# Order of the first loads, and where the second mixer's residual comes from, in a two-layer hybrid encoder kernel

## Chip, cores and metric

The kernel runs on one core of one Trainium2 chip. The metric is the device time of one execution in microseconds (us); lower is better. A profiled execution gives the trace from which all rows below are read.

## The reference

The stream x is 1024 tokens by 1024 channels. Two layers are applied, A and B, and a last norm. Each layer is

```
h = rmsnorm(x)
z = h @ w_in                       # token mixer and 4 memory-attention heads from one projection
x = x + concat(token_mixer(z), memory_attention(z, mem)) @ w_out
x = x + conv_ffn(rmsnorm(x))
...
out = rmsnorm(x)
```

Layer A's token mixer is a gated block of width 768 (u times a spatially mixed v, with a bias `a_b_s`). After layer A one shared K and V and a forget gate (with a bias `b_f` for each of 12 heads) are computed from x. Layer B's token mixer is causal attention with that K, V and a decay. The line that matters most here is the first residual of layer B: the x that is added to the mixer's output is the stream that left layer A's feed-forward part.

## The kernel before

All products are done in float32 precision with split operands: a tile is cast to a rounded high part (ScalarE, ACT) and the remainder is the low part (VectorE, DVE, or GpSimd, POOL): `split_to` (L346, L347), `wconv` for weights (L213 multiplies the gains in, L217 casts, L218 subtracts). TensorE (PE) then runs three products for each pair. Tiles of 128 x 1024 come from one pool of 33 buffers called X.

The program is written as straight code, and a planner orders each engine's instructions by its own model of times. Matmuls are pinned to the order in which they are written while `strict` is set. A load made with `ld` (L184) is pinned behind the load written before it on the same queue as long as `dpin` is set; a load that is not pinned may be moved ahead of loads that were written earlier, if nothing holds it. Nearly all loads and stores are issued from SP's queue, one after the other; a few small ones of the start are issued from ACT's.

**Start.** Written in this order: two tiles of x, the rows of norm gains (on ACT's queue), two weights of the first projection (`ast.load(2)`), six more tiles of x, two of mem, `ws_raw`; then `dpin` is cleared. In a loop over four pairs of x tiles, `x_in(i+1)` transposes and splits the next pair, and `vv_g` multiplies the pair before with the first weight. The first call of `vv_g` asks for the third weight (`m`, 0) too. The bias `bsb` (L1121, eight small broadcasts) and `bf` (L1225, one) are written much later, and not pinned.

**End of layer A.** `ffn` ends with `out_phase`; when a tile of the new stream is whole, `on_done` calls `done_a`, which splits it into `nh`, `nl` and adds its square to a sum. They become `xh`, `xl`, the operands of layer B's projections. `xdram` is a DRAM array that holds the stream in the middle of each layer (`mix_out` writes it, L577, and `load_xT` reads it).

**End of layer B's attention.** After 48 attention steps, `tail` loads the six attention outputs `o` from DRAM (L1607, tiles of the ring `nb`, three buffers), splits each (`split_new`), and between them `merge_next` (L1599) adds `xl` and `xh` on GpSimd to get the residual back. The memory attention runs at the same time: `mem_s` (reduce L478, exponential L481, reciprocal L484, and `normalise` L459 on GpSimd) and `mem_p` (transpose, split, product). `mix_part` multiplies the split `o` with the output weight and adds the residual (L565).

Of the kernel before, what the change touches and what calls it, by code (L numbers as in the profile page):

```python
# [13 lines left out]
ALU = mybir.AluOpType  # L14
AX = mybir.AxisListType

P = 128
# [42 lines left out]
def kernel(  # L60
# [33 lines left out]
    nc = tc.nc  # L94
# [8 lines left out]
    xdram = dp.tile([D, S], F32, name="xdram")  # L103
# [9 lines left out]
    def nm(s):  # L113
        uid[0] += 1
        return f"{s}_{uid[0]}"

    def xt_(dt=F32, shape=(P, S)):
        return xp.tile(list(shape), dt, tag="X", name=nm("X"))
# [7 lines left out]
    def small(n, tag="sm", p=P):  # L126
        return sm.tile([P, n], F32, tag=tag, name=nm(tag))[:p]
# [3 lines left out]
    def f32(ap):  # L131
        return ap.bitcast(F32)
# [48 lines left out]
    dpin = [False]  # L181

    def ld(dst, src):
        ins = nc.sync.dma_start(dst, src)  # L184
        if dpin[0]:
            tc.keep_in_program_order(ins)
# [100 lines left out]
    def proj_tm_g(ws, xh, xl, j, res, width=256):  # L287
        ps = pa()[:, :width]
        res.append(ps)
        for k in range(KT):  # L290
            wh, wl = ws[k // 4]
            for i, (a, b) in enumerate(((xh, wh), (xh, wl), (xl, wh))):
                mm(
                    ps, a[k][:, j * P:(j + 1) * P], b[:, k % 4, :],
                    start=(k == 0 and i == 0), stop=(k == KT - 1 and i == 2),
                )
            yield 324


    def rpow(dst, src, n):  # L300
        nc.gpsimd.tensor_tensor(dst, src, mhalf[:, :n], ALU.pow)
# [31 lines left out]
    def add_square(tp, ssum, src, n, tag="T", bufs=None):  # L333
        if n == 0:
            nc.scalar.activation(ssum, src, AF.Square)
        else:
            sq = tp.tile([P, S], F32, tag=tag, name=nm("sq"), bufs=bufs)
            nc.scalar.activation(sq, src, AF.Square)
            if n == KT - 1:
                nc.vector.tensor_tensor(ssum, ssum, sq, ALU.add)  # L340
            else:
                nc.gpsimd.tensor_tensor(ssum, ssum, sq, ALU.add)

    def split_to(hi, lo, src, g=None):
        if g is None:
            nc.scalar.copy(hi, src)  # L346
            nc.vector.tensor_tensor(lo, src, f32(hi), ALU.subtract)  # L347
        else:
            nc.scalar.activation(hi, src, AF.Copy, scale=g)
            nc.vector.scalar_tensor_tensor(lo, src, g, f32(hi), ALU.mult, ALU.subtract)  # L350

    def split_new(t):
        hi, lo = xt_(F32R), xt_(F32R)
        split_to(hi, lo, t)
        return hi, lo
# [8 lines left out]
    def mem_norm(tp, mtok, jtag, jbufs):  # L364
        rm = small(2, "rt")
        ms = small(2)
        for t in range(2):
            junk = tp.tile([P, D], F32, tag=jtag, name=nm("jk"), bufs=jbufs)
            nc.scalar.activation(junk, mtok[t], AF.Square, accum_out=ms[:, t:t + 1])
        ms2 = small(2)  # L370
        nc.vector.tensor_scalar(ms2, ms, 1.0 / D, EPS, ALU.mult, ALU.add)
        rpow(rm, ms2, 2)
        return rm
# [143 lines left out]
    def drain(g):  # L517
        for _ in g:
            pass
# [32 lines left out]
    def mix_part(ww, ks, mh, ml, xn):  # L552
        wh, wl = ww
        ps = [pa(), pa()]
        for k in ks:
            for i, (a, b) in enumerate(((wh, mh), (wh, ml), (wl, mh))):
                for c in range(NC2):
                    mm(
                        ps[c], a[:, k, :], b[k][:, c * CH:(c + 1) * CH],
                        start=(k == ks[0] and i == 0), stop=(k == ks[-1] and i == 2),  # L560
                    )
                yield 432
        for c in range(NC2):
            cs = slice(c * CH, (c + 1) * CH)
            nc.vector.tensor_tensor(xn[:, cs], ps[c], xn[:, cs], ALU.add)  # L565
# [435 lines left out]
    xh = [xt_(F32R) for _ in range(KT)]  # L1001
    xl = [xt_(F32R) for _ in range(KT)]
    r_a = small(8, "rt")

    def x_in(i):
        ss, s2 = small(2), small(2)
        toks = xtok[2 * i:2 * i + 2]
        for j in range(2):
            junk = tp.tile([P, S], F32, tag="P", name=nm("jk"), bufs=pbufs[0])
            nc.scalar.activation(junk, toks[j], AF.Square, accum_out=ss[:, j:j + 1])  # L1010
        nc.vector.tensor_scalar(s2, ss, 1.0 / D, EPS, ALU.mult, ALU.add)
        rpow(r_a[:, 2 * i:2 * i + 2], s2, 2)
        for k2 in range(KT // 2):
            ps = pa()
            for k in range(2):
                for j in range(2):
                    kk = 2 * k2 + k
                    tr(ps[:, (2 * k + j) * P:(2 * k + j + 1) * P], toks[j][:, kk * P:(kk + 1) * P], ident)
            for k in range(2):
                cs = slice(2 * i * P, (2 * i + 2) * P)  # L1020
                split_to(xh[2 * k2 + k][:, cs], xl[2 * k2 + k][:, cs], ps[:, 2 * k * P:(2 * k + 2) * P])
# [29 lines left out]
    ws_raw = tp.tile([P, 4, P], F32, tag="T2", name="ws_raw", bufs=3)  # L1051
    ld(ws_raw, a_w_s[0].rearrange("g t s -> t g s"))

    dpin[0] = False
    vg = {}
    sv = cp.tile([P, KT, 3], F32, name="sv")

    def vv_square(cc, j):
        junk = tp.tile([P, CH], F32, tag="T2", name=nm("jk"), bufs=t2b[0])
        nc.scalar.activation(  # L1060
            junk[:, :256], vg[cc, j // 4][:, j % 4, :], AF.Square, accum_out=sv[:, j, cc:cc + 1])

    def vv_g(cc, js):
        ws = ast.use(("v", cc), 2)
        for j in js:
            if j % 4 == 0:
                vg[cc, j // 4] = xt_(F32, (P, 4, 256))
            res = []
            yield from proj_tm_g(ws, xh, xl, j, res)
            d = vg[cc, j // 4][:, j % 4, :]  # L1070
            nc.scalar.activation(  # L1071
                d, res[0], AF.Gelu_apprx_tanh if cc == 0 else AF.Copy, scale=r_a[:, j:j + 1])
            if cc == 0:
                vv_square(cc, j)

    for i in range(4):
        if i < 3:
            x_in(i + 1)
        drain(vv_g(0, (2 * i, 2 * i + 1)))
    rm = mem_norm(tp, mtok, "P", pbufs[0])  # L1080
    rb = cp.tile([P, S], F32, name="rb_a", tag="rb", bufs=1)

# [33 lines left out]
    bsb = tp.tile([P, 6, P], F32, tag="bsb", name="bsb", bufs=1)  # L1116
    fgroups = [[(0, 0, P)], [(0, 0, 64), (1, 64, P)], [(1, 0, P)],
               [(2, 0, P)], [(2, 0, 64), (3, 64, P)], [(3, 0, P)]]
    for f in range(6):
        for g, lo_, hi_ in fgroups[f]:  # L1120
            ld(bsb[lo_:hi_, f, :], a_b_s[0, g:g + 1, :].broadcast_to([hi_ - lo_, P]))  # L1121

    memq.append(mem_q(1))

# [76 lines left out]
    xT = {}  # L1201
# [20 lines left out]
        return a[:, :n], a[:, n:], b[:, :n], b[:, n:]  # L1222

    bf = cp.tile([P, 12], F32, name="bf")
    nc.sync.dma_start(bf, b_f.rearrange("(o h) -> o h", o=1).broadcast_to([P, 12]))  # L1225
    nh, nl, ssums = [], [], []

    def done_a(n, xn):
        h, l = xt_(F32R), xt_(F32R)
        split_to(h, l, xn)  # L1230
        nh.append(h)
        nl.append(l)
        if n == 0:
            ssums.append(tp.tile([P, S], F32, tag="T", name=nm("S"), bufs=4))
        add_square(tp, ssums[0], xn, n, "T", 4)
# [7 lines left out]
    def before_last(stage):  # L1243
# [11 lines left out]

    ffn(ops, ssum_a, first, a_ffn_out[0], lambda: conv_cols("cva", a_ffn_conv, a_ffn_conv_b),
        done_a, tp, False, before_last)
    drain(mt_g[0])
    ssum, = ssums
    xh, xl = nh, nl  # L1260
# [194 lines left out]
    for pr in range(5):  # L1455
        p = PSEQ[pr + 1]
        eng = nc.vector if pr == 0 else None
        wst.add(("k", p), *ntile_src(w_kv, p * P), g_kv, None, eng, pr == 0)
        wst.add(("q", p), *ntile_src(w_q, p * P), g_b1, None, eng, pr == 0)
        if pr in (1, 3):  # L1460
            g = GSEQ[(pr + 1) // 2]
# [89 lines left out]
    for pr in range(5):  # L1551
        fills.append((proj_kq(PSEQ[pr + 1]), KQ, 0, 8 * pr + KQD))
        if pr in (1, 3):
            g = GSEQ[(pr + 1) // 2]
# [38 lines left out]

    xT = {}

    def merge_next(eng):
        n = NORD[len(xT)]
        t = xt_()
        eng.tensor_tensor(t, f32(xl[n]), f32(xh[n]), ALU.add)  # L1599
        xT[n] = t  # L1600

    mix = {}

    def tail():
        for i, p in enumerate(PSEQ):
            o = tp.tile([P, S], F32, tag="nb", name=nm("o"), bufs=3)
            nc.sync.dma_start(o, odram[p * P:(p + 1) * P, :])  # L1607
            if i < 5:
                merge_next(nc.gpsimd)
            mix[p] = split_new(o)  # L1610
        while len(xT) < KT:
            merge_next(nc.gpsimd)
        mh, ml = ({p: mix[p][i] for p in PSEQ} for i in range(2))
        for n in NORD[:NPRE]:
            yield from mix_part(wst.use(("o", n), 1)[0], PSEQ, mh, ml, xT[n])

    tg = tail()
    debt = 0.0
    for cost in mem_g:
# [73 lines left out]
```

## Time and profile before

| what | value |
|---|---|
| runs of the kernel | 2258.61 us median of 3 (2258.33 to 2260.14) |
| the profiled execution, own time | 2259.49 us |
| its span, first to last instruction | 2257.7 us |
| PE busy | 2140.5 us, 95% of the span |
| DVE, ACT, POOL busy | 1719.6, 1036.4, 794.0 us |
| granted clock of PE, mean | 0.987 |

The span is what the trace covers; the execution's own time is 1.79 us longer. In the rows below, a time at the start of a line is us from the start of the span; PEld is PE's weight load, SPq and ACTq are the issuing of a transfer by that queue, not the transfer. "[7.23 <-DMA X<-in_x_dram]" at the end of a row says that the engine was idle for 7.23 us before it and that this transfer ended the wait.

### The profile page before, as it was taken

The numbers are of one execution on the slowest core, as the hardware profiler recorded it, in microseconds if no ns is written. First come the engines' busy times: TensorE is split into PE (matmuls) and PEld (weight loads), VectorE is DVE, ScalarE is ACT, GpSimd is POOL, SyncE is SP. The second block draws the span as 40 slices with busy tenths as digits, with TensorE's granted clock in tenths as the row PEclk, the third lists the DMA queues.
The fourth block names the chain that finished last, engine by engine and source line by source line (L and its number), as shares of the span: only waits on it lengthen the run. The fifth ranks groups of instructions, "written<-read, shape, count | busy, mean of one in ns | idle before, by whom it ended". The sixth has DMA issues, their size and how long they took to land.

```text
span 2257.7 us, 29405 instructions
## 1 busy us (share of the span) xinstructions
PE 2140.5 (95%) x10657; PEld 1785.8 (79%) x10657; DVE 1719.6 (76%) x2544; ACT 1036.4 (46%) x1732; POOL 794.0 (35%) x602
## 2 busy tenths in 40 slices
PE   7999999999999999999899999789999999999998
PEld 6997877778777888878788788667777778788886
DVE  4745667888888899566776766785888888887965
ACT  6562344444434434344565555654434444445433
POOL 1311543333333100351545554555333333320023
PEclk9999999999999999999999999999999999999999
DMA  5310322222222675513332333323222222248563
GB/s 175 100 29 29 93 95 66 72 78 85 84 78 81 225 273 177 169 34 93 104 79 81 88 103 81 96 84 103 68 75 84 71 79 84 85 160 278 159 198 120
DMA packets 219165, 243.54 MB, mean 108 GB/s; under 512 B 10074, under 2 KB 155648, under 8 KB 219020
## 3 DMA queue, kind: packets, MB, share of 16 engines
q1 hardware_dynamic: 218880, 241.63, 34.3%
q8 instruction: 84, 1.38, 0.3%
q14 instruction: 61, 0.50, 0.1%
q10 hardware_dynamic: 140, 0.04, 0.0%
HBM read 192.29 MB, written 38.85 MB: 102 GB/s over the span
## 4 chain that ended last, share of the span: by engine, by line
PE 66%; DVE 18%; issue 6%; ACT 5%; POOL 3%; DMA 3%; ACTq 0%; DVEq 0%; POOLq 0%; SPq 0%
PE pa L137 59%; PE pc L137 5%; DVE X L701 4%; DVE X L699 4%; PE pc L143 2%; DVE ws L660 1%; DVE P L1378 1%; DMA nb<-cdram 1%; DVE U L720 1%; DVE X L347 1%; POOL wo L641 1%; DVE X L430 1%; ACT P L1384 1%; POOL wl L218 1%; DVE PTl L347 1%
## 5 line engine op out<-in xcount | busy, mean ns | idle before, releaser
L137 PE MATMUL pa<-X,wo 128*128 128x512 f32 x3696 | 856.8, 392 | 27.1 <-DVE U L720 21.0
L137 PEld LDWEIGHTS pa<-X,wo 128*128 128x128 f32 x3696 | 691.7, 188 | 189.9 <-DVE U L720 37.6
L137 PE MATMUL pa<-X,X 128*128 128x512 f32 (+2 forms) x1868 | 440.1, 379 | 14.3 <-DVE sm L1378 9.1
L137 PEld LDWEIGHTS pa<-X,X 128*128 128x128 f32 x1868 | 340.0, 189 | 83.3 <-DVE sm L1378 9.1
L137 PE MATMUL pa<-X,wh 128*128 128x512 f32 (+1 forms) x1216 | 354.9, 401 | 10.6 <-DVE X L347 8.5
L641 POOL TENSOR_TENSOR wo<-raw,wo 128x512 fp32r<-128x512 f32 x132 | 223.8, 1695 | 319.2 <-ACT wo L639 315.6
L137 PEld LDWEIGHTS pa<-X,wh 128*128 128x128 f32 x1216 | 219.9, 191 | 56.2 <-DVE X L347 11.0
L639 ACT CAST wo<-ws 128x512 fp32r<-128x512 f32 x176 | 109.3, 622 | 300.8 <-PE pa L137 293.3
L798 ACT CAST X<-ro 128x1024 fp32r<-128x1024 f32 (+1 forms) x142 | 131.0, 965 | 175.8 <-DVE ro L806 74.0
L641 POOL TENSOR_TENSOR wo<-ws,wo 128x512 fp32r<-128x512 f32 x88 | 116.3, 1321 | 233.5 <-ACT wo L639 226.9
L137 PE MATMUL pa<-X,wl 128*128 128x512 f32 (+1 forms) x608 | 195.6, 401 | 2.6 <-POOL wl L218 2.5
L799 POOL TENSOR_TENSOR X<-ro,X 128x1024 fp32r<-128x1024 f32 (+1 forms) x24 | 59.5, 2482 | 344.8 <-ACT X L798 336.2
L218 POOL TENSOR_TENSOR wl<-wr,wh 128x1024 fp32r<-128x1024 f32 (+1 forms) x41 | 104.0, 2538 | 183.6 <-ACT wh L217 178.6
L137 PE MATMUL pa<-wh,X 128*128 128x256 f32 (+1 forms) x800 | 167.4, 287 | 0.5 <-ACT X L1071 0.5
L799 DVE TENSOR_TENSOR X<-ro,X 128x1024 fp32r<-128x1024 f32 (+1 forms) x118 | 142.6, 1237 | 31.6 <-ACT X L798 29.2
L137 PEld LDWEIGHTS pa<-wh,X 128*128 128x128 f32 x800 | 132.3, 189 | 2.3 <-ACT X L1071 0.7
L137 PEld LDWEIGHTS pa<-X,wl 128*128 128x128 f32 x608 | 111.0, 191 | 23.0 <-POOL wl L218 2.9
L639 ACT CAST wo<-raw 128x512 fp32r<-128x512 f32 x132 | 81.3, 616 | 95.0 <-PE pa L137 90.3
L347 DVE TENSOR_TENSOR PTl<-pc,PTh 128x512 fp32r<-128x512 f32 (+1 forms) x152 | 90.9, 602 | 36.7 <-ACT PTh L346 35.2
L137 PE MATMUL pa<-wl,X 128*128 128x256 f32 (+1 forms) x400 | 113.6, 284 | 2.2 <-POOL wl L218 2.2
L1384 ACT ACTIVATE P<-P,sm 128x128 f32<-128x128 f32 (+3 forms) x96 | 74.8, 779 | 77.8 <-DVE sm L1378 75.9
L459 POOL TENSOR_SCALAR P<-P,sm 128x128 f32<-128x128 f32 (+3 forms) x96 | 76.3, 795 | 92.6 <-DVE sm L1385 81.4
(196 smaller groups left out, 3337.9 us busy)
## 6 DMA issues: line engine op xcount, KB each, us to landing
ro<-hdram SPq DMA_DIRECT2D x67, 512.0 KB
raw<-in_a_ffn_in_dram SPq DMA_DIRECT2D x44, 512.0 KB
hdram<-X SPq DMA_DIRECT2D x44, 512.0 KB
raw<-in_b_ffn_in_dram SPq DMA_DIRECT2D x44, 512.0 KB
ro<-in_a_ffn_out_dram SPq DMA_DIRECT2D x35, 512.0 KB
ro<-in_b_ffn_out_dram SPq DMA_DIRECT2D x32, 512.0 KB
X<-X SPq DMA_DIRECT2D x80, 128.0 KB
xdram<-X SPq DMA_DIRECT2D x16, 512.0 KB
```

The source lines that it names most:

```text
L137: ins = nc.tensor.matmul(*a, **k)
L143: ins = nc.tensor.transpose(*a)
L218: eng.tensor_tensor(lo, raw, f32(hi), ALU.subtract)
L347: nc.vector.tensor_tensor(lo, src, f32(hi), ALU.subtract)
L459: nc.gpsimd.tensor_scalar(p, p, rinv, 1.0, ALU.mult, ALU.mult)
L639: nc.scalar.copy(h, src)
L641: eng.tensor_tensor(l, src, f32(h), ALU.subtract)
L699: nc.vector.scalar_tensor_tensor(t[:, 1:], h[:, :S - 1], w1, t[:, 1:], ALU.mult, ALU.add)
L701: nc.vector.scalar_tensor_tensor(t[:, 2:], h[:, :S - 2], w0, t[:, 2:], ALU.mult, ALU.add)
L798: nc.scalar.copy(h, src)
L799: (nc.gpsimd if pool else nc.vector).tensor_tensor(l, src, f32(h), ALU.subtract)
L1384: nc.scalar.activation(p[:, :n], p[:, :n], AF.Exp, bias=mn, scale=-1.0, accum_out=rs)
```

## The change

Five edits. The pinning of loads lasts until after the loop over x. The eight broadcasts of `bsb` are issued from ACT's queue, pinned behind what is written before them there (the key splits of the memory attention). `bf` is pinned behind what is written before it on SP's queue. `done_a` stores each finished tile to `xdram`. `tail` loads the residual from `xdram` where it was added up on GpSimd.

```diff
-    dpin[0] = False
     vg = {}
     sv = cp.tile([P, KT, 3], F32, name="sv")
@@
         if i < 3:
             x_in(i + 1)
         drain(vv_g(0, (2 * i, 2 * i + 1)))
+    dpin[0] = False
     rm = mem_norm(tp, mtok, "P", pbufs[0])
@@
     for f in range(6):
         for g, lo_, hi_ in fgroups[f]:
-            ld(bsb[lo_:hi_, f, :], a_b_s[0, g:g + 1, :].broadcast_to([hi_ - lo_, P]))
+            tc.keep_in_program_order(nc.scalar.dma_start(
+                bsb[lo_:hi_, f, :], a_b_s[0, g:g + 1, :].broadcast_to([hi_ - lo_, P])))
@@
     bf = cp.tile([P, 12], F32, name="bf")
-    nc.sync.dma_start(bf, b_f.rearrange("(o h) -> o h", o=1).broadcast_to([P, 12]))
+    tc.keep_in_program_order(
+        nc.sync.dma_start(bf, b_f.rearrange("(o h) -> o h", o=1).broadcast_to([P, 12])))
     nh, nl, ssums = [], [], []

     def done_a(n, xn):
+        nc.sync.dma_start(xdram[n * P:(n + 1) * P, :], xn)
         h, l = xt_(F32R), xt_(F32R)
@@
-    def merge_next(eng):
+    def load_next():
         n = NORD[len(xT)]
-        t = xt_()
-        eng.tensor_tensor(t, f32(xl[n]), f32(xh[n]), ALU.add)
-        xT[n] = t
+        xT[n] = xt_()
+        nc.sync.dma_start(xT[n], xdram[n * P:(n + 1) * P, :])
@@
             if i < 5:
-                merge_next(nc.gpsimd)
+                load_next()
             mix[p] = split_new(o)
         while len(xT) < KT:
-            merge_next(nc.gpsimd)
+            load_next()
```

## Rows read from the trace of the kernel before

**Rows 1.** The page, busy time of each engine over the span.

```profile
PE 2140.5 (95%) x10657; PEld 1785.8 (79%) x10657; DVE 1719.6 (76%) x2544; ACT 1036.4 (46%) x1732; POOL 794.0 (35%) x602
```

**Rows 2.** PE's waits over the span: total us, times, longest.

```profile
PE pa L137 <- DVE U L720: 21.0, 38, 0.6
PE pa L143 <- DMA X<-in_x_dram: 13.7, 4, 7.2
```

**Rows 3.** Timeline of SP's queue at the start: start, us, what.

```profile
1.71 5.20 SPq L184 DMA_DIRECT2D wr<-in_a_w_in_dram  x3
7.62 5.19 SPq L184 DMA_DIRECT2D bsb<-in_a_b_s_dram  x8
13.33 3.12 SPq L184 DMA_DIRECT2D X<-in_x_dram  x6
```

**Rows 4.** Timeline of PE at the start.

```profile
17.89 0.48 PE L143 MATMUL pa<-ident,X 128*128 128x128 f32 x1 [7.23 <-DMA X<-in_x_dram]
19.21 3.46 PE L143 MATMUL pa<-ident,X 128*128 128x128 f32 x15 [0.84 <-DMA X<-in_x_dram]
22.68 0.41 PE L137 MATMUL pa<-wl,X 128*128 128x256 f32 x1
```

**Rows 5.** Timeline of all engines at the start: splitting the first weights.

```profile
9.40 1.04 ACT L1010 ACTIVATE jk<-X 128x1024 f32<-128x1024 f32 x1
16.21 1.22 DVE L218 TENSOR_TENSOR wl<-wr,wh 128x1024 fp32r<-128x1024 f32 x1
16.79 2.85 POOL L218 TENSOR_TENSOR wl<-wr,wh 128x1024 fp32r<-128x1024 f32 x1 [5.25 <-ACT wh L217]
```

**Rows 6.** Windows of the start: busy us by engine, granted clock, DMA share, GB/s.

```profile
15.00:20.00 5.00, 1.27 (x5) 0.98 (x6) 5.00 (x6) 1.78 (x4) 2.85 (x1) 0.50 0.93 353
20.00:25.00 5.00, 5.00 (x31) 5.00 (x30) 2.54 (x4) 4.25 (x7) 0.71 (x1) 0.64 1.03 416
```

**Rows 7.** Timeline of ACT after the memory attention's key splits.

```profile
82.24 1.05 ACT L217 CAST wh<-wr 128x1024 fp32r<-128x1024 f32 x1 [6.84 <-PE pa L137]
```

**Rows 8.** Timeline of SP's queue, and a window, at layer A's end.

```profile
967.27 0.34 SPq L786 DMA_DIRECT2D ro<-hdram  x1
950.00:960.00 10.00, 10.00 (x46) 8.29 (x45) 7.14 (x7) 6.32 (x7) 2.49 (x1) 1.00 0.01 2
```

**Rows 9.** PE's waits from 1436 to 1500.

```profile
PE pa L137 <- DVE X L347: 8.5, 6, 2.6
PE pa L137 <- DVE sm L1378: 5.4, 1, 5.4
PE pc L143 <- DVE sm L484: 1.4, 1, 1.4
```

**Rows 10.** GpSimd's groups from 1430 to 1500: busy us, mean ns, idle before.

```profile
L1599 POOL TENSOR_TENSOR X<-X,X 128x1024 f32<-128x1024 f32 x8 | 20.4, 2558 | 0.0
L459 POOL TENSOR_SCALAR Pm<-Pm,sm 128x256 f32<-128x256 f32 x32 | 16.0, 512 | 21.8 <-DVE sm L484 19.2 <-PE pa L137 2.6
```

**Rows 11.** Timeline of DVE: two splits of attention outputs.

```profile
1464.38 3.33 DVE L347 TENSOR_TENSOR X<-o,X 128x1024 fp32r<-128x1024 f32 x1 [0.20 <-ACT X L346]
1483.34 1.22 DVE L347 TENSOR_TENSOR X<-o,X 128x1024 fp32r<-128x1024 f32 x1
```

**Rows 12.** Line views: L430 over the span (ns min/median/max), L347 from 1464 to 1498.

```profile
L430 DVE TENSOR_TENSOR X<-qf,X x40: 673/690/2722, 66.4 to 1442.2; 64x512 fp32r<-64x512 f32 x40
L347 DVE TENSOR_TENSOR X<-o,X 128x1024 fp32r<-128x1024 f32 x6 | 16.4, 2740 | 0.3 <-ACT X L346 0.2
```

**Rows 13.** Timeline of SP's queue and of ACT: loading and casting the attention outputs.

```profile
1467.74 13.93 SPq L1607 DMA_DIRECT2D o<-odram  x4
1471.21 1.05 ACT L346 CAST X<-o 128x1024 fp32r<-128x1024 f32 x1
```

**Rows 14.** Window of the attention-output splits, columns as in rows 6.

```profile
1464.40:1489.30 24.90, 16.44 (x77) 12.26 (x77) 24.05 (x25) 15.89 (x38) 17.48 (x16) 0.93 0.27 87
```

**Rows 15.** Timeline of GpSimd: the last adds.

```profile
1485.75 8.07 POOL L1599 TENSOR_TENSOR X<-X,X 128x1024 f32<-128x1024 f32 x3
```

## The prediction

> **What bounds the kernel now.** I began with the page: PE is busy for 2140.5 of 2257.7 us [rows 1]. Idle PE time is 117 us in all, so an edit far from PE's gaps is worth little, and one that closes a gap is worth that gap at most. The second view is PE's waits over the span. The largest entry, 21.0 us in 38 short waits, is in the feed-forward loops, which the change does not touch; the next is 13.7 us in 4 waits for tiles of x, the longest 7.2 us [rows 2]. Those are at the start, so the third view is the start's timeline, on SP's queue and on PE. The fourth is PE's waits where `merge_next` runs, 1436 to 1500 us: 8.5 us for L347, 5.4 us for L1378 and 1.4 us for L484 [rows 9]. The last is what GpSimd and DVE do there. The reader should see two different things. At the start the queue is busy with bytes that nobody needs yet. At the end of the attention DVE, not PE, is the bound: 24.05 of 24.90 us busy [rows 14], and GpSimd's adds run in the same stretch.
>
> **Start: loads behind x.** SP issues two weights and a third from 1.71 us, then eight broadcasts for 5.19 us, and reaches the other six tiles of x only at 13.33 us [rows 3] (`bf` fills the 0.52 us between). PE waits 7.23 us for the first of these, 0.84 us for the second, transposes until 22.67 us, and comes to the first product with a low part at 22.68 us [rows 4]. The third weight, the broadcasts and `bf` now stand behind x. SP's first two weights stay. The three weight issues took 5.20 us, which includes waits, so I put the first moved tile where the third weight's issue was, near 6.5 us, and the second where the first broadcast was, 7.62 us. Before, the first tile of this pair took 4.6 us from its issue at 13.33 us to PE's first transpose at 17.89 us [rows 3, 4]; by that the pair starts PE at 11.1 and 12.2 us, against 17.89 and 19.21 us: 7 us earlier. The wires do not forbid it: a tile is 512 KB, 1.26 us at the 416 GB/s of a full stretch [rows 6].
>
> PE does not get all of that, because the weight is late next. Its first low part is done on DVE at 17.43 us and its second on GpSimd at 19.64 us [rows 5]. The product needs the first at once and the second halfway. So the most that can be gained is 22.68 - 17.43 = 5.25 us. The least: the pair's two squares (1.04 us each [rows 5]) and its eight casts, each of a quarter of that size, now compete with the weight on ACT, their remainders on DVE. ACT was idle for 3.2 of the 5 us from 15 on, but DVE was full [rows 6]; if all of the pair's ACT work, 2.1 us of squares and by size as much of casts, goes ahead of the weight, the first low part comes 4.2 to 4.8 us later and 0.5 us is left. For the weight to win speaks that the third weight's own conversion leaves this stretch too. I take 3.5 us, nearer the upper end.
>
> **Start: what the moved loads cost.** The third weight is wanted only after the loop over the four pairs, and lands behind x and mem: hidden by the loop's products. The eight broadcasts move to ACT's queue, pinned behind the key splits. Behind them there, ACT is idle for 6.84 us until PE frees the next weight buffer at 82.24 us [rows 7]. Eight issues at the 0.65 us each that SP needed, 5.19 us [rows 3], fit into that gap. I cost them at nothing; without the gap, what waits behind them is that weight's cast and the memory queries' splits, for at most 5.2 us. `bf` goes to a place where nothing waits for it.
>
> **End of layer A: eight stores.** Each is one issue on SP of about 0.35 us and 512 KB. The first four are ready in the window from 950 to 960 us, where DVE and ACT finish and split these tiles; SP issues its next load at 967.27 us, and the transfer engines are 1% busy in the window [rows 8]. I cost them at nothing. If the planner puts them behind the load at 967.27 us, they still delay no load; ahead of it and late, four tiles of 1.26 us would hold it for 5 us. A tile's buffer is kept until its store has landed, but its square is still running then.
>
> **End of the attention: eight adds become eight loads.** The adds took 20.4 us of GpSimd, 2.56 us each [rows 10]. GpSimd's time is not what counts: DVE's is. A 128 x 1024 split of an attention output takes 1.22 us when no add runs and 3.33 us beside one [rows 11]; the six took 16.4 us, where 6 x 1.22 = 7.3 us would do [rows 12]. A key split L430 takes 0.69 us in the median of 40, and 2.72 us at most [rows 12]; that one lies under the first add, ahead of the L1378 that PE waits 5.4 us for.
>
> By the Trainium skill, page "SBUF — State Buffer", section "Who interferes with whom", a VectorE instruction with two SBUF inputs and a GpSimd instruction that reads SBUF exclude each other for a whole instruction. The trace agrees as far as the adds go (3.33 against 1.22 us). But the rule covers GpSimd's normalisations too, which stay; by it alone the splits would go on losing time, and this is the first rival below.
>
> The sum here: PE's wait for L1378 shrinks by 2.72 - 0.69 = 2.0 us. The waits for L347 are 8.5 us. With the splits short, what is late next is the loading of `o`. SP issued the last four at intervals of (13.93 - 0.33) / 3 = 4.5 us, each as the split before freed its buffer [rows 13]. From issue to cast took 1471.21 - 1467.74 = 3.5 us, the cast 1.05 us [rows 13], the split would take 1.22 us: 5.8 us for a cycle, two buffers in turn, 2.9 us for each. Four times 4.5 - 2.9 = 1.6 us is 6.4 us, and the first split gives 2.1 us: 8.5 us, as much as PE waited. PE's own work, 16.44 of the 24.90 us [rows 14], leaves the same 8.5 us. I take 5.5 us, since the new loads (eight of 1.26 us on the wires, in a stretch whose DMA share is 27% [rows 14]) and GpSimd's normalisations get in between. The wait for L484, 1.4 us, comes behind three adds of 8.07 us in a row [rows 15]; I take 1.0 us. In all 2.0 + 5.5 + 1.0 = 8.5 us. The upper bound is 2.0 + 8.5 + 1.4 = 11.9 us. The lower: a pair of normalisations (2 x 0.51 us [rows 10]) still delays each of seven splits, 7.1 us, and 1.4 to 2 us is left. What follows is full of PE work and moves forward as it is.
>
> **Sum.** 3.5 + 8.5 = 12.0 us. The profiled execution took 2259.49 us, which gives 2247.5 us; it lies 0.88 us above the median of the runs, 2258.61 us, so on that scale 2246.6, rounded to 2247 us.
>
> **Rivals.**
> *Normalisations or late `o` loads take the adds' place.* For: the 32 normalisations keep 16.0 us of GpSimd [rows 10]. Against: each lasts 0.51 us where an add lasted 2.56 us. The tail then gives 2 us, the start 3.5 us: 2253 us.
> *The weight eats the start.* If the planner puts the x pair wholly ahead of the weight, the start gives 0.5 us and the tail its 8.5 us: 2249.6 us; together with the first rival 2256 us, no measurable change.
> *Slower: a load of the residual blocks SP's queue.* The destination of a load comes from the X pool's 33 buffers, of which `xh` and `xl` hold 16 until the last projection of layer B is done. If the planner believes a buffer free earlier than it is, the load stands at the head of the queue, and the query copies, decay broadcasts and attention-output stores behind it wait, and the attention with them. Each us of block is a us of PE at worst. From 12 us of block on the gain is gone; at 20 us the kernel takes 2267 us. Against: the eight adds needed a buffer each from the same pool, and GpSimd was never idle before one [rows 10].
>
> **How the numbers follow.** A change of 0.2%, 4.5 us, is about what a measurement of this kernel can tell from none. Forecast (7 to 17 us gained): 0.66. One of the two milder rivals, 4.5 to 7 us: 0.15. Both: 0.12. Slower rival: 0.07, most of it by more than 0.2%. So faster 0.81, same 0.13, slower 0.06. The bounds of the two terms added are 17.2 us (2241.4) and about 2 us (2256.6). The range runs from 2241 to 2256 us, which leaves out the slower rival and what the bounds miss, about 2 in 10.
>
> **What would show it.** Start: the pair's transposes begin near 11 us instead of 17.89, the first product with a low part comes between 17.4 and 22.2 us (19.2 by my sum), and no long wait of PE follows it. ACT: the eight issues between 75 and 82 us, PE without a wait there. Layer A's end: the first stores before 967 us, no longer wait for `ro<-hdram`. Tail: no L1599; L347 on `o` near 1.2 to 1.7 us; PE's waits for L347 down from 8.5 to about 3 us, for L1378 from 5.4 to 3.4 us. I am wrong if L347 on `o` stays above 2 us, if SP shows a long wait ahead of a load from `xdram`, or if the start gives less than 0.5 us.

## The result, and the profile after

The changed kernel takes 2244.49 us, median of 4 runs (2241.92 to 2246.33); the kernel before, on the same chip, 2258.47 us, median of 4 (2257.85 to 2260.14). The ratio is 0.9940 with a 95% interval of 0.9928 to 0.9952: 14.0 us faster by the medians, 0.6%. 2247 us was predicted, in a range of 2241 to 2256. The profiled execution took 2246.33 us, 13.2 us less than the one of before; all rows of this section are of it.

The engines' busy times on its page answer to [rows 1]: PE does the same 10657 matmuls, and GpSimd has 8 instructions and 20 us less, the adds.

```profile
PE 2144.9 (96%) x10657; PEld 1789.1 (80%) x10657; DVE 1705.9 (76%) x2544; ACT 1035.7 (46%) x1732; POOL 773.6 (34%) x594
```

Both kernels issue the same matmuls in the same order. So the start of the nth matmul in one trace can be set against the start of the nth in the other, and the difference, the lead of the changed kernel, shows where the time goes. Worked out from both traces (us):

| matmul, start before | start after | lead | what lies there |
|---|---|---|---|
| 17.9 | 10.4 | 7.5 | first transpose of the second x pair |
| 22.7 | 17.4 | 5.3 | first product with a low part of the weight |
| 31.0 | 26.2 | 4.8 | products of the first pairs |
| 84.4 | 80.2 | 4.2 | memory attention |
| 93.5 | 90.4 | 3.1 | low part of a weight, behind PE's wait of 1.8 us |
| 984.5 | 981.5 | 3.0 | end of layer A |
| 1006.5 | 1004.6 | 1.8 | layer B's first weights |
| 1012.7 | 1009.3 | 3.5 | the same stretch |
| 1305.4 | 1302.2 | 3.2 | attention of layer B |
| 1443.3 | 1437.8 | 5.5 | behind the wait for L1381 |
| 1467.8 | 1460.2 | 7.6 | first split of an attention output |
| 1496.9 | 1485.2 | 11.7 | last of them |
| 1529.1 | 1516.1 | 13.0 | behind a wait for a weight (2.5 us before, 1.3 after); kept to the end |

The start gives some 3 us and the end of the attention 9.8 us. Between them the lead goes up and down by a us or two and ends where it was.

**Start.** SP's queue, as in [rows 3]: start, us, what. The six tiles of x are issued from 6.62 us where they were issued from 13.33, and the third weight stands last.

```profile
1.71 0.98 SPq L184 DMA_DIRECT2D wr<-in_a_w_in_dram  x2
6.62 3.95 SPq L184 DMA_DIRECT2D X<-in_x_dram  x6
12.21 1.01 SPq L184 DMA_DIRECT2D wr<-in_a_w_in_dram  x1
```

PE's timeline, against [rows 4]. The transposes begin at 10.42 and 11.95 us, and the first product with a low part (`wl`) at 17.37 us, behind a wait of 0.82 us for the weight's split: the weight is late next.

```profile
10.42 0.47 PE L143 MATMUL pa<-ident,X 128*128 128x128 f32 x1
11.95 3.46 PE L143 MATMUL pa<-ident,X 128*128 128x128 f32 x15 [1.05 <-DMA X<-in_x_dram]
...
17.37 0.58 PE L137 MATMUL pa<-wl,X 128*128 128x256 f32 x1 [0.82 <-DVE wl L218]
```

The windows of the same stretch, against [rows 6]: DVE, full before, has air.

```profile
15.00:20.00 5.00, 3.59 (x15) 2.93 (x15) 3.57 (x7) 4.80 (x10) 3.22 (x2) 1.00 1.03 401
20.00:25.00 5.00, 5.00 (x42) 5.00 (x42) 2.68 (x8) 4.98 (x14) 1.07 (x2) 1.00 1.11 313
```

The clock column reads 1.00 here where it read 0.50 and 0.64, but that is not PE's pace. This trace has no record of the clock before 20.8 us, and a stretch without a record reads 1.00. The transposes tell: 15 take 3.46 us from 11.95 us, exactly as in [rows 4] at a clock of 0.50, and a little later 16 take 1.91 us. PE's products are 0.21 us apart until 20.7 us and 0.12 us behind it. So PE ran at the half clock at the start of this kernel too.

```profile
24.56 1.91 PE L143 MATMUL pa<-ident,X 128*128 128x128 f32 x16
```

**The broadcasts.** ACT's timeline, against [rows 7]: the eight issues do lie in ACT's gap, 69.65 to 75.53 us. But DVE's timeline shows that of the three weights which SP began to load at 68.20 us the last is now late: DVE waits 2.33 us for it. The delay does not reach PE by that weight itself. DVE's next work, a pass over the memory queries (L447), stands behind it, ACT waits 1.72 us for that pass, and behind ACT's queries and exponentials stands the cast of the second of the three weights (86.64 us). GpSimd works out its low part from 87.94 us, and PE waits 1.8 us for that; before the change it waited 0.7 us there. The last two lines are PE's waits from 40 to 120 us, of the kernel before and of the changed one.

```profile
69.65 0.92 ACTq L1121 DMA_DIRECT2D bsb<-in_a_b_s_dram  x2
...
70.61 4.92 ACTq L1121 DMA_DIRECT2D bsb<-in_a_b_s_dram  x6
77.33 1.05 ACT L217 CAST wh<-wr 128x1024 fp32r<-128x1024 f32 x1 [6.85 <-DMA bsb<-in_a_b_s_dram]
```

```profile
78.23 1.23 DVE L213 TENSOR_TENSOR wr<-wr,norms 128x1024 f32<-128x1024 f32 x1 [2.33 <-DMA wr<-in_a_w_in_dram]
```

```profile
80.09 2.38 ACT L429 CAST X<-qf 64x512 fp32r<-64x512 f32 x4 [1.72 <-DVE qf L447]
87.94 2.37 POOL L218 TENSOR_TENSOR wl<-wr,wh 128x1024 fp32r<-128x1024 f32 x1
```

```profile
PE pa L137 <- POOL wl L218: 0.7, 1, 0.7
```

```profile
PE pa L137 <- POOL wl L218: 1.8, 1, 1.8
```

**End of layer A.** SP's queue, against [rows 8]: four stores are issued from 949.31 us, long before the next load.

```profile
949.31 3.41 SPq L1231 DMA_DIRECT2D xdram<-X  x4
963.64 0.32 SPq L786 DMA_DIRECT2D ro<-hdram  x1
```

**End of the attention.** PE's waits from 1425 to 1489 us, against [rows 9] (L1381 is the L1378 of before): the 5.4 us are 3.3, the 8.5 us for L347 are 1.0, the wait for L484 is gone, and a new one, 2.5 us, is for a cast of an attention output.

```profile
PE pa L137 <- DVE sm L1381: 3.3, 1, 3.3
PE pa L137 <- ACT X L346: 2.5, 3, 1.9
PE pc L143 <- ACT PD L1436: 1.9, 2, 1.6
PE pa L137 <- DVE X L347: 1.0, 2, 0.5
```

DVE's groups from 1454 to 1487 us, against [rows 12]: the six splits take 7.3 us, 1222 ns each, where they took 16.4 us. Key splits just ahead, DVE's timeline: four in 3.91 us, none of 2.72 us.

```profile
L347 DVE TENSOR_TENSOR X<-o,X 128x1024 fp32r<-128x1024 f32 x6 | 7.3, 1222 | 3.2 <-ACT X L346 3.1
```

```profile
1433.47 3.91 DVE L430 TENSOR_TENSOR X<-qf,X 64x512 fp32r<-64x512 f32 x4
```

SP's queue, against [rows 13]: the attention outputs are loaded every 3.2 us but for one, where it was 4.5 us; the loads of the residual lie between them.

```profile
1460.14 0.32 SPq L1609 DMA_DIRECT2D o<-odram  x1
...
1463.35 0.32 SPq L1609 DMA_DIRECT2D o<-odram  x1
...
1466.46 0.32 SPq L1609 DMA_DIRECT2D o<-odram  x1
...
1471.67 0.32 SPq L1609 DMA_DIRECT2D o<-odram  x1
1472.04 1.37 SPq L1602 DMA_DIRECT2D X<-xdram  x3
```

### The profile page after: what moved, and what is told of

It is laid out like the page before. It is cut to its first block, busy times and chain, and to the rows that moved or that the text cites. A ratio compares the mean times of both kernels' runs of the same rounds, so it can differ in the third digit from the quotient of the medians.

```text
span 2244.6 us, 29445 instructions
## 1 busy us (share of the span) xinstructions
PE 2144.9 (96%) x10657; PEld 1789.1 (80%) x10657; DVE 1705.9 (76%) x2544; ACT 1035.7 (46%) x1732; POOL 773.6 (34%) x594
## 4 chain that ended last, share of the span: by engine, by line
PE 35%; DVE 9%; issue 3%; ACT 3%; DMA 2%; POOL 1%; DVEq 0%; POOLq 0%; ACTq 0%; SPq 0%
PE pa L137 31%; PE pc L137 2%; DVE X L701 2%; PE pc L143 2%; DVE X L699 2%; DVE P L1381 1%; DMA nb<-cdram 1%; ACT P L1387 1%; DVE ws L660 1%; DVE U L720 1%; DMA wr<-in_b_w_q_dram 0%; DVE X L430 0%; ACT PTh L346 0%; DVE PTl L347 0%; ACT X L429 0%
## 5 line engine op out<-in xcount | busy, mean ns | idle before, releaser
L137 PE MATMUL pa<-X,wo 128*128 128x512 f32 x3696 | 857.1, 392 | 26.9 <-DVE U L720 20.8
L347 DVE TENSOR_TENSOR PTl<-pc,PTh 128x512 fp32r<-128x512 f32 (+1 forms) x152 | 90.8, 602 | 38.9 <-ACT PTh L346 37.2
```

The source lines that it names most:

```text
L137: ins = nc.tensor.matmul(*a, **k)
```

## The experiments

The theory: GpSimd's adds held DVE up and with it PE, some 10 us; the earlier x gives some 3 us; the moved broadcasts take a part of it back, as they delay a weight. Against it stand: that the residual's buffers or the stores matter, not the adds; that the gain of the start is one of its two halves alone; and that the late `o` loads eat part of the tail. Medians are of the kernel's own runs, ratios are to the kernel before run beside it; its median was 2258.15, 2258.77 or 2258.60 us. A gain in us is worked out from the ratio, unless medians are named; the two differ by up to 2.4 us.

### Each half by itself

The diff was cut in two. `e1_start_only` has the three edits of the start alone, `e2_residual_only` the store in `done_a` and `load_next` alone.

> Only the start's edits (loads pinned longer, small broadcasts moved); the residual is still added up on GpSimd. Theory A, the two halves are independent and add up: 3.5 us faster than before (2.5 to 4.5), and the timeline of the end of attention is that of before, with L347 on the attention outputs near 2.7 us. Rival B, the halves help each other through the planner: under 1.5 us, and the sum of this run's and the next run's gains falls short of the whole 14 us by over 3 us.

> Only the stores to xdram and the loads in place of the adds; the start is that of before. Theory A: 9.5 to 10.5 us faster than before, L347 on the attention outputs at 1.22 us, PE's first waits unchanged (7.2 us for x). Rival B: under 8 us.

The residual alone: 2247.79 us, ratio 0.9956 (0.9944 to 0.9968), 9.9 us faster; PE's waits are those of the changed kernel there (3.3 us for L1379, its L1381; 1.3 us for L347). The start alone: 2256.61 us, ratio 0.9996 (0.9988 to 1.0005), 0.9 us faster, which is not told from none. Its trace has a lead of 5.4 us at 17 us, 3.5 us at 90 us and 2.8 us at the end. So the tail's 9.9 us are confirmed by time; of the start's 3 us the trace speaks, while the interval allows a gain of 2.7 us at most. A part of it goes again at 172 us in that trace: PE waits 1.8 us there in both kernels, but here the granted clock is 0.50 for 3.4 us behind the wait, and the lead falls from 3.5 to 1.9 us. `e2_residual_only`, whose start is that of before, loses the same 1.6 us there, so that loss is not the start's edit. The halves sum to 10.8 us; the whole gave 13.6 us on one chip (14.0 by the medians) and, run again beside other kernels, 2246.75 us, ratio 0.9952 (0.9939 to 0.9965), 10.8 us:

> The changed kernel itself, for comparison on the same chip with the three that follow. Theory: 10 to 14 us faster than before; the first runs differed by 4.4 us among themselves, so a few us of that are the stretches of half clock, which fall differently in each run.

### The start taken apart

`e3_weight_only` only clears `dpin` later; the broadcasts and `bf` stay as they were. `e4_small_only` leaves the weight ahead of x and only moves the small loads.

```diff
 # e3_weight_only, on the kernel before
-    dpin[0] = False
...
+    dpin[0] = False          # after the loop over x
 # e4_small_only, on the kernel before
+            tc.keep_in_program_order(nc.scalar.dma_start(bsb..., a_b_s...))
+    tc.keep_in_program_order(nc.sync.dma_start(bf, ...))
```

> Only the pinning is prolonged, so only the third weight moves behind x; the eight broadcasts and bf are as before, not pinned, on SP's queue. Theory A, the small broadcasts are what held x back (5.7 us of SP's queue against one weight's issue): they stay ahead of x, PE's wait for x shrinks by 1 to 2 us and the time by 0 to 1.5 us. Rival B, the third weight with its 512 KB held x back: 3 to 5 us faster.

> Only the broadcasts and bf are moved; the third weight still goes ahead of x. Theory A: the pair of x starts PE near 12 to 13.5 us, the first product with a low part comes at 17.5 to 19 us as in the changed kernel, and the time falls by 2.5 to 4 us. Rival B: PE still waits until 16 us or more for x and the time falls by less than 1.5 us.

The weight alone: 2258.41 us, ratio 0.9997 (0.9988 to 1.0006); PE's second x pair starts only 0.4 us earlier, at 17.47 us, since the broadcasts still go ahead of it:

```profile
17.47 0.48 PE L143 MATMUL pa<-ident,X 128*128 128x128 f32 x1 [7.14 <-DMA X<-in_x_dram]
```

The small loads alone: 2261.06 us, ratio 1.0016 (1.0007 to 1.0024), slower by 3.6 us. That I had not foreseen. The windows of that kernel's trace show how:

```profile
20.00:25.00 5.00, 4.18 (x35) 3.98 (x34) 2.64 (x4) 4.14 (x7) 0.70 (x1) 1.00 1.04 324
25.00:30.00 5.00, 2.34 (x15) 2.16 (x16) 2.68 (x8) 4.98 (x14) 0.69 (x1) 0.90 0.29 81
30.00:35.00 5.00, 4.31 (x21) 3.91 (x20) 0.58 (x3) 4.99 (x15) 0.70 (x1) 0.50 0.00 0
```

PE comes to its first product with a low part with a lead of 5.1 us, but from 25 us on it has 2.34 us of work in 5 us while ACT is full (4.98 us), and after that the granted clock is 0.50, 1.2 GHz, for some 7 us. By 38 us the lead is a loss of 2.0 us. What held PE is ACT, in its timeline: it stood idle for 3.80 us ahead of the third weight's cast, which needs DVE's product with the gains. That product took 3.07 us from 17.75 us, where it takes 1.22 us by itself: GpSimd's subtraction for another weight ran beside it until 19.74 us.

```profile
20.86 1.05 ACT L217 CAST wh<-wr 128x1024 fp32r<-128x1024 f32 x1 [3.80 <-DVE wr L213]
21.81 1.06 ACT L1010 ACTIVATE jk<-X 128x1024 f32<-128x1024 f32 x1
```

The squares and casts of the next x pairs stand behind it in ACT's order, and begin at 21.81 us. In the changed kernel the third weight is cast at 33.32 us and the squares begin at 16.77 us. The cast is where it was before the change, but there the pair was not there either; with the pair early it is a hole. So by the traces the two halves need each other: the small loads let x come early, the weight's later load keeps ACT free for it. The times do not show that: `e3_weight_only` and `e1_start_only`, which has both halves, are told neither from each other nor from the kernel before. Nor are the 3.6 us of `e4_small_only` this hole alone: in its trace the loss is 2.0 us at 70 us and 4.8 us at 100 us, behind the broadcasts.

### The broadcasts moved out of the weight's way

`e7_late_bias` is the changed kernel with the `bsb` loop written after the memory attention's last product, where the broadcasts are issued at 151.83 us.

```diff
-    for f in range(6):
-        for g, lo_, hi_ in fgroups[f]:
-            tc.keep_in_program_order(nc.scalar.dma_start(bsb..., a_b_s...))
     memq.append(mem_q(1))
...
+    # the same loop, after the memory attention's last product
```

> The changed kernel with the eight broadcasts issued from ACT after the memory attention (near 140 us) instead of behind the key splits (near 70 us). Theory A, the broadcasts share the wires with three weights that SP issues at the same time, the third weight lands late and DVE, then PE wait for it: PE's wait of 1.8 us near 89 us falls to 0.7 us or less and the lead at 95 us is 4.5 to 5 us instead of 3.1; 1 to 2 us faster than the changed kernel. Rival B, ACT's own time for the eight issues is what costs: the lead at 95 us is kept, but is lost again behind the issues near 140 us.

Its DVE waits 0.56 us for the weight instead of 2.33 us:

```profile
75.57 1.22 DVE L213 TENSOR_TENSOR wr<-wr,norms 128x1024 f32<-128x1024 f32 x1 [0.56 <-DMA wr<-in_a_w_in_dram]
```

PE's wait for `wl` is 0.7 us, as before the change, and the lead stays at 5.1 us from 38 to 170 us. In the changed kernel it falls between 70 and 100 us, from 4.9 to 3.1 us in the first trace and from 5.0 to 2.1 us in that of `after_again`. So the broadcasts are what made the weight late. Nine kernels' traces here have the broadcasts in this place, and the fall has two sizes. In four it is 1.4 to 1.8 us. In five, `after_again` among them, PE's wait is followed by 3.4 us at a granted clock of 0.50, and the fall is 2.8 to 3.0 us. In `e7_late_bias` and `e9_both` the lead doesn't fall there. The window behind the wait, of `after_again` (the clock, 0.66, is the third column from the end):

```profile
90.00:95.00 5.00, 5.00 (x31) 5.00 (x32) 4.09 (x7) 2.36 (x9) 3.30 (x6) 0.66 0.73 206
```

ACT's cast stays behind a gap of 6.85 us in both, so it was not ACT's time that they took. The windows from 75 to 80 us show the rest, first of the changed kernel, then of `e7_late_bias`; the last two columns are the DMA share and GB/s. Without the broadcasts the transfers are over by 75 us; with them they run on, at 122 GB/s.

```profile
75.00:80.00 5.00, 4.68 (x28) 3.95 (x27) 2.67 (x4) 1.05 (x1) 0.00 (x0) 1.00 0.37 122
```

```profile
75.00:80.00 5.00, 5.00 (x34) 4.52 (x33) 3.81 (x7) 2.80 (x5) 0.00 (x0) 1.00 0.03 7
```

By the Trainium skill, page "DMA: Bandwidth & Descriptors", section "Issuing engines are not separate DMA queues", transfers started by different engines run on the same 16 DMA engines and interleave; another issuer saves only the issuing time. The rows agree. In time the kernel took 2244.36 us, ratio 0.9947 (0.9934 to 0.9960): a median 2.4 us below the changed kernel run beside it, with intervals that overlap. The wait is shown; its price, 1.4 to 3.0 us, is shown by the traces alone.

### The adds put back, beside the loads

`e5_adds_back`, `e6_touch` and `e11_one_input` are the changed kernel with one more GpSimd instruction for each residual tile, whose result nobody reads: the whole add, the add of 8 columns, and a scaling of the whole tile with one input. Loads and buffers stay.

```diff
         nc.sync.dma_start(xT[n], xdram[n * P:(n + 1) * P, :])
+        nc.gpsimd.tensor_tensor(xl[n], f32(xl[n]), f32(xh[n]), ALU.add)              # e5
+        nc.gpsimd.tensor_tensor(xl[n][:, :8], ..., ALU.add)                          # e6
+        nc.gpsimd.tensor_scalar(xl[n], f32(xl[n]), mhalf[:, 0:1], 1.0, ALU.mult, ALU.mult)  # e11
```

> The changed kernel, with GpSimd's eight adds of xl and xh put back beside the loads; their results are thrown away. Theory A, the adds hold up DVE's splits: L347 on the attention outputs is near 2.5 us again instead of 1.22, PE's waits for L347 between 1425 and 1500 us are over 6 us again, and 8 to 11 us of the gain are gone (2254 to 2258 us). Rival B, the loads instead of the adds shorten a chain (the residual is there earlier): nothing changes, 2244 to 2248 us.

> As the run before, but each add covers only 8 of 1024 columns: xl and xh keep their 16 buffers as long as with the full adds, and GpSimd has next to nothing to do. Theory A: as the changed kernel, 2244 to 2248 us, L347 at 1.22 us. Rival C, the gain came from the 16 buffers that come free earlier: 2252 us or more, with L347 at 1.22 us but casts that wait for buffers.

> As the run with the full adds, but GpSimd scales xl in place by a column (one input in SBUF, 128x1024, near 1.5 us each) instead of adding xh; the results are thrown away. If any reading by GpSimd holds up DVE's splits: those that fall beside a pass take 2 to 3 us, and 3 to 7 us of the gain are lost. If only instructions with two inputs do: L347 stays at 1.22 us and the time is that of the changed kernel.

With the adds back: 2256.12 us, ratio 0.9987 (0.9978 to 0.9995). All but some 3 us of the gain is gone, though the loads are still there; the start's edits are in this kernel too. With adds of 8 columns, from 1408 to 1431 us where the full ones stand from 1406 to 1441 us: 2245.07 us, ratio 0.9941 (0.9929 to 0.9953), all of the gain. So the tail's gain is the adds' size, not the loads, and not how long a buffer is held.

But the place was not the one I had in mind. PE's waits of `e5_adds_back` from 1425 to 1505 us, and DVE's splits of the attention outputs from 1445 to 1500 us:

```profile
PE pa L137 <- DVE sm L1381: 7.9, 2, 7.2
...
PE pa L137 <- DVE X L347: 1.2, 3, 0.5
```

A wait just ahead of that window belongs to it, PE's for L1388: 6.3 us, where the changed kernel has 2.2 us (waits from 1395 to 1505 us).

```profile
PE pc L143 <- DVE sm L1388: 6.3, 1, 6.3
```

```profile
L347 DVE TENSOR_TENSOR X<-o,X 128x1024 fp32r<-128x1024 f32 x6 | 7.3, 1223 | 1.5 <-ACT X L346 1.2
```

The splits of `o` are as short as in the changed kernel: the adds, no longer tied to them, ran earlier, from 1406 us on. What is long there are key splits. The line view of L430 (ns min/median/max), against [rows 12], and GpSimd's timeline:

```profile
L430 DVE TENSOR_TENSOR X<-qf,X x40: 675/690/5607, 61.8 to 1448.0; 64x512 fp32r<-64x512 f32 x40
```

```profile
1436.20 4.75 POOL L1603 TENSOR_TENSOR X<-X,X 128x1024 fp32r<-128x1024 f32 x2
1440.91 1.03 POOL L459 TENSOR_SCALAR P<-P,sm 128x896 f32<-128x896 f32 x1
1441.89 2.35 POOL L218 TENSOR_TENSOR wl<-wr,wh 128x1024 fp32r<-128x1024 f32 x1
1444.19 0.73 POOL L1357 TENSOR_TENSOR md<-nb,cmask 128x256 f32<-128x256 f32 x1
1444.89 1.13 POOL L459 TENSOR_SCALAR P<-P,sm 128x1024 f32<-128x1024 f32 x1
```

The split of 5.61 us starts at 1440.95 us, 0.04 us behind a normalisation, and lasts until GpSimd's row of instructions, each at the heel of the other since the adds had put them off, is over. The lead falls by 9.1 us from 1400 to 1443 us in this trace. So the adds cost some 10 us in both places where they were tried, by DVE's two-input splits and by GpSimd's own queue behind them; the runs do not part these two. By the Trainium skill, page "SBUF — State Buffer", section "Who interferes with whom", the one that comes second is blocked fully; the trace agrees: a split of 0.69 us beside an add ends 0.54 us behind the add's end, whenever it began. That one split stayed blocked through four GpSimd instructions in a row is more than the page says. It is one case: other splits of this trace got their turn between two GpSimd instructions that followed each other at once, and why this one did not stays open.

The scaling, 1.12 us each, 1.55 for the two that run beside key splits: 2247.46 us, ratio 0.9957 (0.9943 to 0.9972). None of the passes fell beside a split of `o` (1.22 us there too). But two fell beside key splits, which have two inputs as well, and those splits took 1.50 us instead of 0.69, with the same 0.54 us between the end of the pass and theirs: four key splits take 5.55 us where `e6_touch` has 3.93 us, and PE's wait for L1388 is 3.8 instead of 2.2 us. So a one-input pass delays a two-input split too, only for less long. In its trace the lead falls by 2.8 us from 1400 to 1430 us, a part of it by 3.4 us at a clock of 0.50; the median is 2.4 us above that of `e6_touch`, with intervals that overlap.

```profile
1406.50 5.55 DVE L430 TENSOR_TENSOR X<-qf,X 64x512 fp32r<-64x512 f32 x4
```

### The loads of the attention outputs

The wait of 1.9 us for a cast came with one `o` load that took 6.0 us from issue to cast (1463.35 to 1469.34 us). `e8_rest_last` issues two of the residual's loads between the `o` loads and pins the other six behind the last; `e9_both` adds the late broadcasts of `e7_late_bias`.

```diff
-            if i < 5:
+            if i < 2:
                 load_next()
...
-            load_next()
+            load_next(True)      # kept in program order
```

> The changed kernel with only two of the eight residual loads between the loads of the attention outputs and the other six pinned behind the last of those. Theory A, the residual loads hold up the attention outputs on the wires (6.0 us from issue to cast where 3.5 us would do): every cast follows its issue by 3.0 to 4.0 us, PE's wait of 1.9 us near 1470 us goes, 1.5 to 2.5 us faster than the changed kernel. Rival B, ACT and DVE are the limit there: the casts come no earlier and the time stays.

> The two edits before together on the changed kernel. Theory A: their gains add up, 2.5 to 4.5 us faster than the changed kernel. Rival B: the same time as the changed kernel within 1.5 us.

`e8_rest_last`: 2244.48 us, ratio 0.9944 (0.9931 to 0.9958), casts of the last four 3.6 to 3.9 us behind their issue, PE's wait for L346 down to 0.6 us. But the changed kernel run beside it (`after_again`), with its loads in the old order, had 0.9 us there, with casts 4.0 to 4.4 us behind their issue. The wait of 1.9 us was one late transfer of one execution; the residual's loads delay the casts by half a us or so, and no harm to the time can be told from these runs. `e9_both`: 2243.00 us, ratio 0.9938 (0.9923 to 0.9953), the best median, 15.8 us below the kernel before and 3.8 us below the changed kernel beside it; the intervals overlap here too.

### The stores left out

`e10_no_store` is the changed kernel without the store in `done_a`: its residual is the mid-layer stream, another than the reference's.

```diff
     def done_a(n, xn):
-        nc.sync.dma_start(xdram[n * P:(n + 1) * P, :], xn)
```

> The changed kernel without the eight stores at layer A's end; the residual that is loaded is then the stream of the middle of layer A, so the output is another. Theory A, the stores cost nothing: within 1.5 us of the changed kernel. Rival B, they delay layer B's first loads or hold buffers: 1.5 to 3 us faster, and the lead that PE loses at 985 us (0.6 to 1.2 us) stays.

2246.84 us, ratio 0.9947 (0.9933 to 0.9961): not faster than with them. The dip of the lead near 985 us that I had put down to the second four stores is there as well. The window from 980 to 990 us of this kernel has the clock (0.83) that the changed kernel has in it; the kernel before has 1.00 there, and so has `after_again`, with the stores, whose lead does not dip.

```profile
980.00:990.00 10.00, 8.71 (x31) 6.80 (x32) 6.23 (x8) 5.06 (x5) 5.07 (x4) 0.83 0.16 52
```

## Why the prediction was right

**Start, 3.5 us predicted.** The x pair came at 10.4 and 11.95 us (11.1 and 12.2 predicted) and the weight was late next, as said. The first product with a low part came at 17.37 us, the earliest end of what I had allowed, and not at 19.2 us: a lead of 5.3 us. That term was too small: with the third weight's conversion gone from the stretch DVE was busy for 3.57 of 5 us where I had seen it full, and the weight won over the pair's squares on ACT, which began at 16.77 us, behind its cast at 15.55 us. The half clock of [rows 6], which I had not priced, did not go: PE ran at half pace until 20.7 us, and the lead falls from 5.3 to 4.8 us by 31 us.

**Broadcasts, nothing predicted.** This is the step that failed. I argued that the issues fit into ACT's gap; they do. I did not ask what was on the wires then: the three weights of 512 KB that SP issues at 68 us. That took 1.8 us of the lead by 100 us in the first trace and 2.9 us in that of `after_again`, and `e7_late_bias` shows that it comes back without them. In the first trace the two errors cancel in the start's sum, 3.1 us for 3.5, and that is luck: in the other 2.1 us are left. In time the start alone gave 0.9 us, with an interval that ends at 2.7, below 3.5 us.

**Stores and `bf`, nothing predicted.** Right: `e10_no_store` gains nothing, and no load of SP's queue waited behind the first four.

**Tail, 8.5 us predicted, 9.9 us by `e2_residual_only`, 9.8 us by the trace's lead.** The mechanism held, and its parts: the wait for L1378 went from 5.4 to 3.3 us (3.4 predicted); the splits are 1.22 us long (1.2 to 1.7); the loads of `o` come every 3.2 us (2.9); PE's waits for the splits and casts together are 3.5 us (3). The wait for L484 went whole, 1.4 us where I took 1.0. From 1400 to 1497 us the lead grows by 8.5 us in the first trace and by 10.7 us in that of `after_again`, which has neither the late transfer nor the half clock that the first has at 1471 us; that the first meets the 8.5 us is luck too. The last 1.3 us of the first trace come at 1529 us, in a wait for a weight's low part, where I had said that what follows only moves forward. So the tail gave more than its term and the start less, and the whole, 13.6 us and 10.8 us by the ratios, lies on either side of 12.0 us.

**The rivals.** The normalisations didn't take the adds' place beside the splits of `o`: they stay in the program, but none ran beside one of the six, which are all 1.22 us. They do act where they meet a key split: in the changed kernel one at 1434.45 us, beside a normalisation, takes 1.50 us against 0.69 in the median, part of what is left of the wait for L1381. Beside an add of 2.81 us one took 2.72 us: in both cases the split ends 0.54 us behind the end of the GpSimd instruction. So normalisations do delay a split that they meet, as the first rival had it; they cost little because they are short and few of them meet one. The weight didn't eat the start. No load from `xdram` blocked SP's queue.

## What to carry over

A transfer moved to another engine's queue gives up its place in the issuing order but not on the wires: look at which bulk load is in flight there, not at the issuing engine's gap alone. Work that is off the critical path on GpSimd is not free while DVE splits tiles beside it: here 20 us of adds cost some 10 us of the whole, and a reload of 512 KB for each add cost nothing that could be measured. An edit with two parts can need both: by the traces one half brought x only 0.4 us earlier, and the other was 3.6 us slower; the gain of both together is seen in the traces and not told by the times. A sum that comes out near can hide terms that are off: compare the trace with each of them.

## What the runs showed of the hardware

- An earlier start can cost: in `e4_small_only` PE had its first products 5.1 us sooner, then 2.34 us of work in 5 us, and then about 7 us at a granted clock of 0.50.
- A 64x512 two-input split on DVE that begins beside a GpSimd instruction ends 0.54 us behind the end of that instruction, one-input (1.50 us in all) or two-input (2.72 us); by itself it takes 0.69 us. A 128x1024 split beside an add ends 1.08 us behind the add's end (2.65 to 3.36 us in the kernel before; 1.22 by itself). A GpSimd queue without gaps held one 64x512 split for 5.61 us; others got their turn in such a queue.
- Stretches at a clock of 0.50 move from one execution to the next: in the first trace of the changed kernel, but not in that of the kernel before, near 980 and 1274 us, in both near 336 and 1250 us. Each of these follows a wait of PE. The same wait need not do it: all fourteen traces have a wait of 1.6 to 1.8 us between 170 and 180 us, and in six of them the clock is 0.50 for 3.4 us behind it, for 1.6 us of the lead. Leads of a us or two that come and go between 980 and 1280 us lie at such stretches, and runs of one kernel are 3 to 11 us apart. That is why medians settle the tail but not the parts of the start.
